# Layer 1's modulation vectors made beside the first parts of two SwiGLU stages; wider context products; more raw buffers in the last SwiGLU

## The chip, the cores and the metric

The kernel runs on one core of a Trainium2 chip. Its engines work side by side, each on its own queue in order: PE (TensorE, matrix products; PEld is its weight load), DVE (VectorE), ACT (ScalarE), POOL (GpSimd) and SP (SyncE, which here only issues transfers). The metric is the device time of one execution in microseconds.

## The reference

Two layers over 512 latent tokens of width 1024 (the noisy x) and 256 context tokens. Each layer is a SwiGLU half step, a mixer, and a second SwiGLU half step:

```
mod_l = silu(c) @ w_mod[i] + b_mod[i]          # 9 vectors of 1024 for the latent stream
mod_c = silu(c_ctx) @ w_mod[i] + b_mod[i]      # and 9 for the context stream
h = rmsnorm(s, g) * (1 + mod[k0 + 1]) + mod[k0]
s = s + 0.5 * mod[k0 + 2] * ((silu(h @ w1) * (h @ w3)) @ w2)     # d_ff = 2816
x = x + mod[5] * mixer(...)                    # layer 0: S5 and pooling; layer 1: gated DeltaNet
```

In layer 1 the context needs only vectors 0 to 4, the latent stream all nine. All arithmetic is in float32: a product of two float32 matrices is three PE products of high and low halves (high × high, high × low, low × high), so weights and activations are split into a high part (copied on ACT) and a low part (a subtraction on DVE).

## The kernel before, in words

The streams x and ctx stand together in SBUF as xT, 128 partitions × 8 blocks × 768 tokens (512 latent, 256 context), 24 KB of each partition, 3 MB in all. Six stages follow one another: ffn01, mixer0, ffn02 (layer 0), ffn11, mixer1, ffn12 (layer 1); the code numbers them ph 1 to 6.

The function ffn7 does the stages 3, 4 and 6. Its first part makes h @ w1, h @ w3 by a scheme of seven block products instead of eight. A unit is one block of d_ff: 7 × 12 = 84 PE products of 384 columns (256 in ffn12, where there is no context). Ahead of the units stands eight(), which does the first four slabs with plain products while the sums of blocks (combine(): tiles hr, h7h, h7l) are still being made on DVE and ACT; its inner ctx() does the context columns, two products of 128 columns for the two halves of a block. unit_prep() gets one unit's weights ready: raw slabs of 512 KB come by SP's queue, ACT makes whi and sh, DVE makes wlo, sl and sums in place. A raw buffer (three of them, RAWS) is loaded again as soon as DVE's sl has read it. The finished units (cffn, with the gate product gkffn for two of them) are stored to DRAM by POOL's queue (gdffn<-cffn).

The second part multiplies by w2 in chunks of units: first units 19 and 20, which have stayed in SBUF (gk), then 0 to 8, 9 to 15, and a last one. It loads the stored units again on POOL's queue (grffn<-gdffn), splits them (ghffn on ACT, glffn on DVE), and DVE adds each result, times the gate, to xT (xT<-ps,gate,xT). PE writes to eight banks; a block of the output takes two of them (one for x, one for ctx) until DVE has added it.

The modulation vectors of layer 1 come from mods(): a slab of w_mod (wm, 512 KB, by POOL's queue), and for each stream one DVE product with a running sum (mscr<-wm,cbc, 128x1024), where cbc holds silu(c) and silu(c_ctx) in every partition. The thread aside() makes them in the second parts of ffn02 (vectors 1, 0, 2, 4, both streams) and of ffn11 (3 for both streams, then 5, 7, 6, 8 for the latent stream), in a pool that has room only there; the main thread waits for ("mods", ph) before the last chunk, because that memory is needed for h.

What stands where on each queue is worked out in advance by class Flow, which runs the threads against a cost model: each has a priority (main work 0 to 4, aside 5), and mods() has a pace in ns (MPS) for its slabs. All engine calls go through one proxy, so the profile has one line, L207, for all of them; tile names tell them apart. In the profile's names the buffer numbers are left out.

Of the kernel before, what the change touches and what calls it, by code (L numbers as in the profile page):

```python
# [10 lines left out]
F32 = mybir.dt.float32  # L11
# [7 lines left out]
P = 128  # L19
# [50 lines left out]
MPS = 4000.0  # L70
RAWS = 3
# [212 lines left out]
class Kern:  # L284
# [47 lines left out]
    def start_stream(self, order):  # L332
        self.order = order
        self.raw, self.sl = {}, {}
        self.pos = 0
        for i in range(RAWS):
            self.slab_dma(i)
        for i in range(3):
            self.slab_prep(i)

    def slab_dma(self, i):
        if i >= len(self.order):
            return
        src, j = self.order[i]
        n = self.A[src].shape[2]
        t = self.slabp.tile([P, 1024], F32, name=f"raw{i}", tag="raw", bufs=RAWS)
        self.nc.sync.dma_start(t[:, :n], self.A[src][j])
        self.raw[i] = (t, n)

    def slab_prep(self, i):  # L350

        if i >= len(self.order):
            return
        src, j = self.order[i]
        if src in UNITS and 2 * CU <= j < 2 * NF:
            if j % 2 == 0:
                self.flow.spawn(self.unit_prep(i), name="slab", prio=3)
            else:
                self.flow.set("slot", i)
            return  # L360

        def prep():
# [12 lines left out]
            self.slab_dma(i + RAWS)  # L375
            self.flow.set("raw", i + RAWS)

        def g():
            if i >= RAWS:
                yield ("raw", i)  # L380
            yield from prep()
        self.flow.spawn(g(), name="slab", prio=3)


    def unit_prep(self, i):
# [47 lines left out]
        for k in range(2):  # L433
            self.slab_dma(i + RAWS + k)
            flow.set("raw", i + RAWS + k)
# [85 lines left out]
    def mods(self, layer, items, bufs, pace, streams=lambda k: (0, 1), beside=None, side="right"):  # L521
# [3 lines left out]
        with self.tc.tile_pool(name=f"mod{layer}{flat[0][1]}", bufs=1, side=side) as mp:  # L525
            cbc = mp.tile([P, 2, D], F32, name="cbc")
# [3 lines left out]
            def load(i):  # L530
                if i < len(flat):
                    _, k, d = flat[i]
                    w[i] = mp.tile([P, D], F32, name=f"wm{layer}_{k}_{d}", tag="wm", bufs=bufs)
                    nc.gpsimd.dma_start(w[i], A["wmod"][layer, 8 * k + d])
# [10 lines left out]
            for i, (gi, k, d) in enumerate(flat):  # L545
                yield self.flow.landed(w[i])
# [3 lines left out]
                for s in streams(k):  # L550
                    scr = mp.tile([P, D], BF16, name="mscr", tag="mscr", bufs=1)
# [15 lines left out]
    def mods_of(self, layer, ks, streams=lambda k: (0, 1), pace=5000.0, beside=None, side="right"):  # L567
        return self.mods(layer, [[(k, d) for d in range(KD)] for k in ks], 2, pace, streams, beside, side)
# [364 lines left out]
    def ffn7(self, layer, which, with_ctx, ph, nxt):  # L933
# [10 lines left out]
        cs, cp = self.cs, self.cp  # L944
        ss = ExitStack()
# [4 lines left out]
        def eight():  # L950
# [4 lines left out]
            def mm(out, u, k, i, cs):  # L955

                w, r = ws[u], blk[k // 4][i]
                t = (k + 4) % 8 if u % 2 == 0 else k
                self.mm3(out, w, t, self.h, (ALL, r, k % 4, cs), k == 0, k == KD - 1)

            def x(us, i):
                for k in range(KD):
                    yield from self.flag("h", ph, i, k)
                    for u in us:
                        mm(px[u][:, i * HN:(i + 1) * HN], u, k, i, slice(0, HN))
                        yield "PE"

            def ctx(u):
# [237 lines left out]
        for c in range(3):  # L1206
            fs, nf = WCH[c], len(WCH[c])
            for d in range(KD):
                px = yield from self.get()
                pc = (yield from self.get()) if with_ctx else None  # L1210
                for i in range(nf):
# [12 lines left out]
                    yield "PE"  # L1224
                yield from self.flag("mod", layer, 3 * n + 2, d)
# [4 lines left out]
        if ph in (3, 4):  # L1230
            yield ("mods", ph)
# [22 lines left out]
        es[1].close()  # L1254

# [1321 lines left out]
    def aside(self):  # L2577
# [9 lines left out]
        yield ("second", 3)  # L2587
        yield from self.mods_of(1, (1, 0, 2, 4), pace=MPS, side="left")
        self.flow.set("mods", 3)
        yield ("second", 4)  # L2590
        yield from self.mods_of(1, (3,), pace=MPS, side="left")
        yield from self.mods_of(1, (5, 7, 6, 8), one, pace=MPS / 2, side="left")
        self.flow.set("mods", 4)
# [188 lines left out]
```

## Time and profile before

| | |
|---|---|
| median of 3 runs | 3070.82 us (3068.51 to 3077.32) |
| profiled execution, its own time | 3083.76 us |
| its span, mean granted clock | 3082.0 us, 0.957 |
| PE busy | 2830.7 us (92%) |
| DVE busy | 2073.8 us (67%) |
| ACT busy | 1244.5 us (40%) |
| ffn02: first part, second part | 1005 to 1298, 1298 to 1504 us |
| ffn11: first part, second part | 1557 to 1852, 1852 to 2065 us |
| ffn12: first part, second part | 2712 to 2940, 2940 to 3067 us |

The time outside the span is 1.8 us. The chain that ended last tells which engine set the end; a window gives one stretch: its length, the busy time of PE, PEld, DVE, ACT and POOL with the number of instructions in brackets, then the granted PE clock as a share of full speed, the busy share of the DMA engines and GB/s. The clock has two levels, 1.2 and 2.4 GHz, so 0.5 is the lower one throughout. A wait names the engine that stood, what it was about to write, and the engine and tile that released it. A PE product is listed from its issue to its modelled end, and the next one starts before that, so the distance of starts is what one costs.

### The profile page before, as it was taken

What the parts mean: (1) busy time and instruction counts of PE and PEld (TensorE: products, weight loads), DVE (VectorE), ACT (ScalarE), POOL (GpSimd) and SP (SyncE); (2) the same over time, 40 slices, a digit from 0 to 9 for tenths busy, and PEclk for the clock granted to TensorE, in tenths of its full rate; (3) what the DMA queues carried; (4) which work ended last, traced back from release to release, by engine and by line L of the source; (5) the groups of instructions that cost most, each with busy time, mean ns of one, the idle gap of its engine ahead of it and who ended that gap; (6) DMA issues with size and microseconds to landing.
All of it is one profiled execution on the core that took longest, in us unless ns stands there. A gap on an engine that the chain in (4) does not pass through costs nothing.

```text
span 3082.0 us, 47486 instructions
## 1 busy us (share of the span) xinstructions
PE 2830.7 (92%) x18572; PEld 2569.6 (83%) x18572; DVE 2073.8 (67%) x3941; ACT 1244.5 (40%) x2464; POOL 707.6 (23%) x1206
## 2 busy tenths in 40 slices
PE   7999899999999999999799999988678888889998
PEld 3778778898888999988799998787567777789977
DVE  6888763366737666588766667667667676687854
ACT  3221212234235444421544443126565766455532
POOL 1343530031311000011200001132664474100011
PEclk9999999999997999999899999989889999899999
DMA  6545442223411223366132326642111123234442
GB/s 226 169 151 171 161 125 64 62 65 92 117 50 36 98 94 99 107 232 196 42 101 95 99 98 222 225 146 78 56 42 45 36 100 111 72 93 123 131 156 74
DMA packets 98673, 343.86 MB, mean 112 GB/s; under 512 B 12384, under 2 KB 16128, under 8 KB 97296
## 3 DMA queue, kind: packets, MB, share of 16 engines
q1 hardware_dynamic: 57552, 192.12, 19.5%
q0 software_dynamic: 37568, 144.51, 14.3%
q10 hardware_dynamic: 3328, 4.20, 0.4%
q8 instruction: 146, 2.39, 0.3%
q14 instruction: 79, 0.65, 0.1%
HBM read 301.81 MB, written 38.96 MB: 111 GB/s over the span
## 4 chain that ended last, share of the span: by engine, by line
PE 60%; DVE 10%; DMA 9%; POOL 9%; issue 8%; ACT 3%; POOLq 0%; DVEq 0%; SPq 0%; ACTq 0%
PE ps L207 60%; DMA wm<-in_wmod_dram 3%; POOL xm L207 2%; POOL s5l L207 2%; POOL z L207 2%; DVE mscr L207 2%; DMA E<-gd 2%; DMA grffn<-gdffn 1%; POOL s5u L207 1%; DVE wlo L207 1%; DMA wf<-in_wmodf_dram 1%; DVE xT L207 1%; DMA z<-in_s5c_dram 1%; DMA og<-ogd 1%; DVE rsq_r L207 1%
## 5 line engine op out<-in xcount | busy, mean ns | idle before, releaser
L207 DVE TENSOR_TENSOR wlo<-raw,whi 128x1024 fp32r<-128x1024 f32 (+1 forms) x310 | 353.6, 1142 | 305.0 <-ACT whi L207 304.6
L207 ACT ACTIVATE whi<-raw 128x1024 fp32r<-128x1024 f32 (+1 forms) x324 | 315.9, 977 | 583.8 <-PE ps L207 530.3
L207 PE MATMUL ps<-hhi,whi 128*128 128x256 f32 (+1 forms) x1304 | 457.2, 351 | 0.5 <-ACT gg L207 0.5
L207 PE MATMUL ps<-hlo,whi 128*128 128x256 f32 (+1 forms) x1304 | 441.3, 338 | 1.1 <-DVE hlo L207 1.1
L207 PE MATMUL ps<-hhi,wlo 128*128 128x256 f32 (+1 forms) x1304 | 440.4, 338 | 2.1 <-DVE wlo L207 1.4
L207 DVE SCALAR_TENSOR_TENSOR mscr<-wm,cbc 128x1024 bf16<-128x1024 f32 x224 | 285.6, 1275 | 62.2 <-DMA wm<-in_wmod_dram 52.8
L207 PE MATMUL ps<-ghffn,whi 128*128 128x256 f32 (+1 forms) x896 | 302.2, 337 | 25.0 <-DVE xT L207 18.2
L207 PE MATMUL ps<-h7h,wlo 128*128 128x384 f32 (+2 forms) x1040 | 319.7, 315 | 4.0 <-DVE wlo L207 4.0
L207 PE MATMUL ps<-h7h,whi 128*128 128x384 f32 (+2 forms) x1040 | 321.4, 317 | 1.2 <-ACT cffn L207 0.8
L207 PE MATMUL ps<-h7h,sl 128*128 128x384 f32 (+1 forms) x960 | 295.0, 319 | 14.1 <-DVE sl L207 14.1
L207 PE MATMUL ps<-glffn,whi 128*128 128x256 f32 (+1 forms) x896 | 301.1, 336 | 1.3 <-DVE glffn L207 1.3
L207 PE MATMUL ps<-ghffn,wlo 128*128 128x256 f32 (+1 forms) x896 | 299.6, 334 | 1.4 <-DVE wlo L207 1.4
L207 PE MATMUL ps<-h7h,sh 128*128 128x384 f32 (+1 forms) x960 | 295.9, 319 | 4.2 <-ACT cffn L207 4.2
L207 PEld LDWEIGHTS ps<-hhi,wlo 128*128 128x128 f32 x1304 | 251.2, 193 | 31.3 <-DVE wlo L207 1.8
L207 PEld LDWEIGHTS ps<-hhi,whi 128*128 128x128 f32 x1304 | 252.2, 193 | 27.3 <-issue 1.4
L207 PEld LDWEIGHTS ps<-hlo,whi 128*128 128x128 f32 x1304 | 252.5, 194 | 25.1 <-DVE hlo L207 1.8
L207 DVE SCALAR_TENSOR_TENSOR xT<-ps,gate,xT 128x256 f32<-128x256 f32 (+1 forms) x352 | 194.2, 577 | 84.6 <-PE ps L207 82.9
L207 PE MATMUL ps<-h7l,whi 128*128 128x384 f32 (+2 forms) x1040 | 240.1, 315 | 2.3 <-DVE h7l L207 2.3
L207 PEld LDWEIGHTS ps<-ghffn,whi 128*128 128x128 f32 x896 | 172.9, 193 | 44.8 <-DVE xT L207 16.5
L207 PEld LDWEIGHTS ps<-h7h,wlo 128*128 128x128 f32 x1040 | 205.7, 198 | 4.5 <-DVE wlo L207 4.4
L207 PEld LDWEIGHTS ps<-h7h,whi 128*128 128x128 f32 x1040 | 206.1, 198 | 2.0 <-ACT cffn L207 1.2
L207 PEld LDWEIGHTS ps<-h7h,sl 128*128 128x128 f32 x960 | 180.7, 188 | 16.4 <-DVE sl L207 16.3
(343 smaller groups left out, 6184.8 us busy)
## 6 DMA issues: line engine op xcount, KB each, us to landing
raw<-in_ffn_dram SPq DMA_DIRECT2D x264, 512.0 KB
wm<-in_wmod_dram POOLq DMA_DIRECT2D x128, 512.0 KB, 4.0
raw<-in_gin_dram SPq DMA_DIRECT2D x33, 512.0 KB
grffn<-gdffn POOLq DMA_DIRECT2D x40, 384.0 KB, 4.5
gdffn<-cffn POOLq DMA_DIRECT2D x36, 384.0 KB, 2.6
wf<-in_wmodf_dram POOLq DMA_DIRECT2D x16, 512.0 KB, 7.8
E<-gd SPq DMA_DIRECT2D x16, 384.0 KB
grffn<-gdffn POOLq DMA_DIRECT2D x20, 256.0 KB, 4.0
```

Of the source, the lines that this page charges most:

```text
L207: r = f(*a, **k)
```

## The change

There are three edits. First, mods_in_x(): once combine() has read xT, POOL writes xT to DRAM (xd), and its memory serves as cbc, three slab buffers and the product's output. In ffn02's first part the vectors 1, 0, 2 are made (pace 9000 ns), in ffn11's first part 4 and 3 for both streams (4500 ns) and 5, 7, 6, 8 for one (2700 ns). Then POOL loads xT back, and the second part waits for ("x", ph) ahead of its first addition to xT. The second parts make no vectors any more. Second, ctx() does both halves of a block in one product of 256 columns, a strided slice of h. Third, ffn12 opens a raw buffer pool of its own with five buffers; slab_dma() counts its slabs itself.

```diff
-MPS = 4000.0
-RAWS = 3
+MPS = 9000.0
...
+        self.rawp, self.raws, self.rawpos = self.slabp, 3, 0
+        for _ in range(self.raws):
+            self.slab_dma()
...
+    def mods_in_x(self, ph, parts):
+
+        nc, flow = self.nc, self.flow
+        xd = self.dram.tile([P, KD, NT], F32, name=f"xd{ph}")
+        yield ("combined", ph)
+        nc.gpsimd.dma_start(xd, self.xT)
+        for ks, streams, pace in parts:
+            yield from self.mods(1, [[(k, d) for d in range(KD)] for k in ks], 3, pace, streams,
+                                 at=self.xT.rearrange("p a c -> p (a c)"))
+        nc.gpsimd.dma_start(self.xT, xd)
+        flow.set("x", ph)
...
+                cbc = at[:, :2 * D].rearrange("p (a c) -> p a c", a=2)
...
+                        w[i] = at[:, (2 + i % bufs) * D:(3 + i % bufs) * D]
...
-                    scr = mp.tile([P, D], BF16, name="mscr", tag="mscr", bufs=1)
+                    scr = mp.tile([P, D], BF16, name="mscr", tag="mscr", bufs=1) if at is None else at[:, 5 * D:]
...
+        if ph == 6:
+            self.rawp, self.raws = rs.enter_context(tc.tile_pool(name="raws", bufs=1, side=SIDES[ph][1])), 5
+            for _ in range(2):
+                self.slab_dma()
...
-                for i in range(2):
-                    for k in range(KD):
-                        yield from self.flag("h", ph, 2, k)
-                        o = 2 * HN * (u % 2)
-                        mm(cb[f][:, (u % 2) * HN + i * P:(u % 2) * HN + (i + 1) * P], u, k, i, slice(HN, HN + P))
-                        if k % 2:
-                            yield "PE"
+                for k in range(KD):
+                    yield from self.flag("h", ph, 2, k)
+                    r = blk[k // 4]
+                    mm(cb[f][:, (u % 2) * HN:(u % 2 + 1) * HN].rearrange("p (a c) -> p a c", a=2), u, k,
+                       slice(r[0], r[1] + 1, r[1] - r[0]), slice(HN, HN + P))
+                    if k % 2:
+                        yield "PE"
...
+                if ph != 6 and ("x", ph) not in flow.flags:
+                    yield ("x", ph)
                 yield from self.flag("mod", layer, 3 * n + 2, d)
...
-        if ph in (3, 4):
-            yield ("mods", ph)
...
-        yield ("second", 3)
-        yield from self.mods_of(1, (1, 0, 2, 4), pace=MPS, side="left")
...
+        both = lambda k: (0, 1)
+        yield from self.mods_in_x(3, [((1, 0, 2), both, MPS)])
+        yield from self.mods_in_x(4, [((4, 3), both, 0.5 * MPS), ((5, 7, 6, 8), one, 0.3 * MPS)])
```

The first place is DVE's queue at the end of ffn02's second part, before (mscr is a product for a modulation vector, x2 two in a row, xT<-ps,gate,xT an addition to the stream):

```order
1505 L207 SCALAR_TENSOR_TENSOR mscr,modv_75<-wm_4_2_12950,cbc 128x1024 x2
1506 L207 SCALAR_TENSOR_TENSOR mscr,modv_75<-wm_4_3_12968,cbc 128x1024 x2
1507 L207 SCALAR_TENSOR_TENSOR mscr,modv_75<-wm_4_4_12990,cbc 128x1024 x2
1508 L207 SCALAR_TENSOR_TENSOR mscr,modv_75<-wm_4_5_12996,cbc 128x1024 x2
1509 L207 SCALAR_TENSOR_TENSOR mscr,modv_75<-wm_4_6_13002,cbc 128x1024 x2
1510 L207 SCALAR_TENSOR_TENSOR mscr,modv_75<-wm_4_7_13008,cbc 128x1024 x2
1511 L207 TENSOR_TENSOR modv_75<-modv_75,vecs 128x8
1512 L207 SCALAR_TENSOR_TENSOR normA<-modv_75,vecs 128x8
1513 L207 TENSOR_TENSOR modv_75<-modv_75,vecs 128x8
1514 L207 SCALAR_TENSOR_TENSOR normA<-modv_75,vecs 128x8
1515 L207 SCALAR_TENSOR_TENSOR xT<-ps_13035,gate,xT 128x256
```

The same place in the change:

```order
1519 L206 TENSOR_TENSOR wlo_12735<-raw_12564,whi_12734 128x1024
1520 L206 SCALAR_TENSOR_TENSOR xT<-ps_12694,gate,xT 128x512
1521 L206 SCALAR_TENSOR_TENSOR xT<-ps_12695,gate,xT 128x256
1522 L206 TENSOR_TENSOR wlo_12793<-raw_12622,whi_12792 128x1024
1523 L206 SCALAR_TENSOR_TENSOR xT<-ps_12746,gate,xT 128x512
1524 L206 SCALAR_TENSOR_TENSOR xT<-ps_12747,gate,xT 128x256
1525 L206 SCALAR_TENSOR_TENSOR xT<-ps_12812,gate,xT 128x256
1526 L206 SCALAR_TENSOR_TENSOR xT<-ps_12827,gate,xT 128x256
1527 L206 SCALAR_TENSOR_TENSOR xT<-ps_12842,gate,xT 128x256
```

The twelve products that stood ahead of the additions of the last chunk are gone from here; only the low halves of slabs stand between the additions.

The second place is POOL's queue where ffn11's first part ends, before:

```order
377 L207 DMA gdffn_13489<-cffn_17_15993 128x768
378 L207 DMA gdffn_13489<-cffn_18_16117 128x768
379 L207 DMA grffn_16599<-gdffn_13489 128x768
380 L207 DMA grffn_16605<-gdffn_13489 128x768
381 L207 DMA grffn_16617<-gdffn_13489 128x768
382 L207 DMA gdffn_13489<-cffn_21_16494 128x768
383 L207 DMA grffn_16621<-gdffn_13489 128x768
384 L207 DMA grffn_16635<-gdffn_13489 128x768
385 L207 DMA grffn_16642<-gdffn_13489 128x768
386 L207 DMA grffn_16650<-gdffn_13489 128x768
```

In the change (xT<-in_wmod_dram is a slab's load into the memory of xT):

```order
380 L206 DMA gdffn_13275<-cffn_17_15767 128x768
381 L206 DMA xT<-in_wmod_dram 128x1024 x4
382 L206 DMA gdffn_13275<-cffn_18_15900 128x768
383 L206 DMA xT<-in_wmod_dram 128x1024 x7
384 L206 DMA xT<-xd_11434 128x6144
385 L206 DMA grffn_16413<-gdffn_13275 128x768
386 L206 DMA grffn_16419<-gdffn_13275 128x768
387 L206 DMA grffn_16430<-gdffn_13275 128x768
388 L206 DMA grffn_16432<-gdffn_13275 128x768
389 L206 DMA gdffn_13275<-cffn_21_16299 128x768
390 L206 DMA grffn_16444<-gdffn_13275 128x768
```

Loads of modulation slabs now stand among the stores of the last units, and the reload of xT directly ahead of the first loads of stored units.

The third place is DVE's queue in eight() of ffn11, before (wlo is the low half of a slab, the one in row 1645 that of the fourth slab; hr and h7l of 128x4x128 are sums of context blocks):

```order
1641 L207 TENSOR_TENSOR h7l<-hr_13032,h7h 128x4x256
1642 L207 TENSOR_TENSOR wlo_13969<-raw_13544,whi_13968 128x1024
1643 L207 TENSOR_TENSOR raw_13544<-raw_13544,raw_13547 128x512
1644 L207 TENSOR_TENSOR raw_13547<-raw_13547 128x512
1645 L207 TENSOR_TENSOR wlo_13966<-raw_13246,whi_13965 128x1024
1646 L207 TENSOR_TENSOR wlo_13973<-raw_13547,whi_13972 128x512
1647 L207 TENSOR_TENSOR raw_13547<-raw_13544,raw_13547 128x512
1648 L207 TENSOR_TENSOR raw_13544<-raw_13544,raw_13547 128x512
1649 L207 TENSOR_TENSOR hr_13031<-hr_13031,hr_13032 128x4x128
1650 L207 TENSOR_TENSOR sl_0_14006<-raw_13547,sh_0_14005 128x1024
1651 L207 TENSOR_TENSOR hr_13032<-hr_13034,hr_13032 128x4x128
1652 L207 TENSOR_TENSOR sl_1_14016<-raw_13544,sh_1_14015 128x1024
```

In the change:

```order
1649 L206 TENSOR_TENSOR h7l<-hr_12809,h7h 128x4x256
1650 L206 TENSOR_TENSOR hr_12808<-hr_12808,hr_12809 128x4x128
1651 L206 TENSOR_TENSOR hr_12809<-hr_12811,hr_12809 128x4x128
1652 L206 SCALAR_TENSOR_TENSOR hr_12811<-hr_12808,hr_12811 128x4x128
1653 L206 TENSOR_TENSOR aaffn_13589<-aaffn_13589,ps_13582 128x2x128
1654 L206 SCALAR_TENSOR_TENSOR hr_12810<-hr_12811,hr_12810 128x4x128
1655 L206 TENSOR_TENSOR h7l<-hr_12811,h7h 128x4x128
1656 L206 TENSOR_TENSOR h7l<-hr_12808,h7h 128x4x128
1657 L206 TENSOR_TENSOR h7l<-hr_12809,h7h 128x4x128
1658 L206 TENSOR_TENSOR wlo_13683<-raw_13030,whi_13682 128x1024
1659 L206 TENSOR_TENSOR wlo_13689<-raw_13306,whi_13688 128x1024
1660 L206 TENSOR_TENSOR raw_13306<-raw_13306,raw_13343 128x512
```

The sums of context blocks now stand ahead of the low half of the fourth slab (row 1658) and of those that follow. PE's own order changes only by the merged context products and a few neighbours, and SP's is the same.

## Rows read from the trace of the kernel before

**Rows 1.** The page's chain that ended last, by engine.

```profile
PE 60%; DVE 10%; DMA 9%; POOL 9%; issue 8%; ACT 3%; POOLq 0%; DVEq 0%; SPq 0%; ACTq 0%
```

**Rows 2.** Windows: us, busy us of each engine (instructions), clock, DMA share, GB/s.

```profile
1005.00:1298.00 293.00, 293.00 (x1685) 292.47 (x1685) 188.24 (x258) 130.30 (x202) 9.72 (x18) 1.00 0.30 97
1557.00:1852.00 295.00, 293.34 (x1685) 292.49 (x1684) 189.68 (x260) 130.11 (x202) 9.72 (x18) 1.00 0.29 96
1298.00:1504.00 206.00, 192.27 (x1172) 171.90 (x1170) 165.04 (x286) 54.01 (x76) 41.68 (x72) 0.97 0.56 181
1852.00:2065.00 213.00, 198.30 (x1171) 175.61 (x1170) 144.10 (x240) 54.06 (x71) 50.06 (x81) 0.94 0.59 200
```

**Rows 3.** Waits of PE, 1852 to 2065: total, times, longest.

```profile
PE ps L207 <- DVE xT L207: 7.7, 3, 4.9
PE ps L207 <- ACT ghffn L207: 6.2, 2, 6.1
```

**Rows 4.** Windows around those three stalls, and an undisturbed stretch.

```profile
1870.00:1945.00 75.00, 75.00 (x429) 65.42 (x428) 54.99 (x84) 18.01 (x17) 13.21 (x25) 1.00 0.70 236
1460.00:1482.00 22.00, 10.78 (x68) 10.57 (x67) 15.98 (x32) 4.99 (x12) 5.96 (x10) 0.69 0.34 105
1945.00:1962.00 17.00, 10.11 (x30) 6.94 (x29) 10.18 (x15) 5.06 (x6) 4.79 (x9) 0.60 0.73 264
2020.00:2041.00 21.00, 14.07 (x84) 13.60 (x83) 14.66 (x27) 3.84 (x9) 4.59 (x7) 0.76 0.44 151
```

**Rows 5.** Timeline, DVE and PE, 1454 to 1475: start, length, [idle before <-releaser].

```profile
1454.70 1.22 DVE L207 SCALAR_TENSOR_TENSOR mscr<-wm,cbc 128x1024 bf16<-128x1024 f32 x1
...
1474.11 0.58 PE L207 MATMUL ps<-ghffn,whi 128*128 128x256 f32 x1 [11.22 <-DVE xT L207]
```

**Rows 6.** Timeline, POOL and ACT, 1946 to 1951.

```profile
1946.54 1.07 POOL L207 DMA_DIRECT2D grffn<-gdffn  x2
...
1950.93 0.84 ACT L207 ACTIVATE ghffn<-grffn 128x768 fp32r<-128x768 f32 x1 [12.60 <-DMA grffn<-gdffn]
```

**Rows 7.** Groups of the page, modulation of the whole run.

```profile
L207 DVE SCALAR_TENSOR_TENSOR mscr<-wm,cbc 128x1024 bf16<-128x1024 f32 x224 | 285.6, 1275 | 62.2 <-DMA wm<-in_wmod_dram 52.8
...
wm<-in_wmod_dram POOLq DMA_DIRECT2D x128, 512.0 KB, 4.0
```

**Rows 8.** Window: spill of x by SP after ffn11, beside other transfers.

```profile
2066.20:2076.00 9.80, 8.34 (x49) 7.59 (x48) 8.94 (x32) 3.63 (x7) 3.70 (x3) 0.73 0.91 323
```

**Rows 9.** Windows: context products, then products of 256 columns.

```profile
961.60:993.50 31.90, 29.77 (x147) 29.44 (x147) 14.27 (x27) 9.52 (x24) 0.60 (x1) 0.55 0.09 30
1529.20:1545.40 16.20, 16.20 (x148) 16.20 (x146) 9.78 (x12) 5.47 (x8) 0.58 (x1) 1.00 0.06 25
2781.00:2788.50 7.50, 7.50 (x66) 7.50 (x65) 5.88 (x10) 4.21 (x8) 0.54 (x1) 1.00 0.49 165
```

**Rows 10.** Timeline, DVE and PE, 1542 to 1547.

```profile
1542.37 1.23 DVE L207 TENSOR_TENSOR wlo<-raw,whi 128x1024 fp32r<-128x1024 f32 x1 [0.33 <-ACT whi L207]
1545.08 1.82 DVE L207 TENSOR_TENSOR wlo<-raw,whi 128x1024 fp32r<-128x1024 f32 x2
...
1546.35 0.39 PE L207 MATMUL ps<-h7h,wlo 128*128 128x256 f32 x1 [0.68 <-DVE wlo L207]
```

**Rows 11.** Window of ffn12's first part.

```profile
2712.00:2940.00 228.00, 210.51 (x1724) 205.58 (x1723) 181.16 (x267) 114.45 (x203) 12.42 (x23) 0.99 0.41 125
```

**Rows 12.** Waits of PE and ACT in it.

```profile
PE ps L207 <- DVE sl L207: 14.1, 10, 2.2
ACT whi L207 <- DMA raw<-in_ffn_dram: 7.6, 10, 2.5
```

**Rows 13.** Timeline of one of these stalls: PE, DVE, ACT.

```profile
2779.28 0.39 PE L207 MATMUL ps<-h7h,sl 128*128 128x256 f32 x1 [1.33 <-DVE sl L207]
...
2779.48 1.22 DVE L207 TENSOR_TENSOR sl<-raw,sh 128x1024 fp32r<-128x1024 f32 x1
...
2782.88 0.63 ACT L207 ACTIVATE whi<-raw 128x512 fp32r<-128x512 f32 x1 [0.20 <-DMA raw<-in_ffn_dram]
```

More of the change, by code (lines that the diff above doesn't have):

```diff
@@ L335, in start_stream, with slab_dma @@
         self.pos = 0
-        for i in range(RAWS):
-            self.slab_dma(i)
+        self.rawp, self.raws, self.rawpos = self.slabp, 3, 0
+        for _ in range(self.raws):
+            self.slab_dma()
         for i in range(3):
             self.slab_prep(i)
-    def slab_dma(self, i):
+    def slab_dma(self):
+        i = self.rawpos
+        self.rawpos += 1
         if i >= len(self.order):
@@ L345, in slab_dma @@
         n = self.A[src].shape[2]
-        t = self.slabp.tile([P, 1024], F32, name=f"raw{i}", tag="raw", bufs=RAWS)
+        t = self.rawp.tile([P, 1024], F32, name=f"raw{i}", tag="raw", bufs=self.raws)
         self.nc.sync.dma_start(t[:, :n], self.A[src][j])
         self.raw[i] = (t, n)
+        self.flow.set("raw", i)
     def slab_prep(self, i):
@@ L374, in prep @@
             self.flow.set("slab", i)
-            self.slab_dma(i + RAWS)
-            self.flow.set("raw", i + RAWS)
+            self.slab_dma()
         def g():
-            if i >= RAWS:
+            if ("raw", i) not in self.flow.flags:
                 yield ("raw", i)
@@ L433, in unit_prep @@
         for k in range(2):
-            self.slab_dma(i + RAWS + k)
-            flow.set("raw", i + RAWS + k)
+            self.slab_dma()
     def slab(self, src, j, ahead=0):
@@ L519, in mod_finish, with mods @@
                 nc.vector.tensor_scalar(self.gate[:, layer, n, s, ds], m, 0.5 if n != 1 else 1.0, None, op0=ALU.mult)
-    def mods(self, layer, items, bufs, pace, streams=lambda k: (0, 1), beside=None, side="right"):
+    def mods_in_x(self, ph, parts):
[8 more added lines that the diff above has]
+        flow.set("x", ph)
+    def mods(self, layer, items, bufs, pace, streams=lambda k: (0, 1), beside=None, at=None):
         nc, A, V = self.nc, self.A, self.nc.vector
         flat = [(gi, k, d) for gi, g in enumerate(items) for k, d in g]
-        with self.tc.tile_pool(name=f"mod{layer}{flat[0][1]}", bufs=1, side=side) as mp:
-            cbc = mp.tile([P, 2, D], F32, name="cbc")
+        with ExitStack() as es:
+            if at is None:
+                mp = es.enter_context(self.tc.tile_pool(name=f"mod{layer}{flat[0][1]}", bufs=1, side="right"))
+                cbc = mp.tile([P, 2, D], F32, name="cbc")
+            else:
+                cbc = at[:, :2 * D].rearrange("p (a c) -> p a c", a=2)
             nc.gpsimd.dma_start(cbc, bass.AP(tensor=A["cc"].tensor, offset=A["cc"].offset, ap=[[0, P], [D, 2], [1, D]]))
@@ L532, in load @@
                     _, k, d = flat[i]
-                    w[i] = mp.tile([P, D], F32, name=f"wm{layer}_{k}_{d}", tag="wm", bufs=bufs)
+                    if at is None:
+                        w[i] = mp.tile([P, D], F32, name=f"wm{layer}_{k}_{d}", tag="wm", bufs=bufs)
+                    else:
+                        w[i] = at[:, (2 + i % bufs) * D:(3 + i % bufs) * D]
                     nc.gpsimd.dma_start(w[i], A["wmod"][layer, 8 * k + d])
@@ L545, in mods @@
             for i, (gi, k, d) in enumerate(flat):
-                yield self.flow.landed(w[i])
+                yield self.flow.landed(w[i]) if at is None else self.flow.ready(w[i], "vector")
                 while self.busy:
@@ L565, in mods, with mods_of @@
                 yield ("s5",)
-    def mods_of(self, layer, ks, streams=lambda k: (0, 1), pace=5000.0, beside=None, side="right"):
-        return self.mods(layer, [[(k, d) for d in range(KD)] for k in ks], 2, pace, streams, beside, side)
+    def mods_of(self, layer, ks, streams=lambda k: (0, 1), pace=5000.0, beside=None):
+        return self.mods(layer, [[(k, d) for d in range(KD)] for k in ks], 2, pace, streams, beside)
     def ring(self, tag):
@@ L944, in ffn7 @@
         cs, cp = self.cs, self.cp
+        rs = ExitStack()
+        if ph == 6:
+            self.rawp, self.raws = rs.enter_context(tc.tile_pool(name="raws", bufs=1, side=SIDES[ph][1])), 5
+            for _ in range(2):
+                self.slab_dma()
         ss = ExitStack()
@@ L953, in eight, with mm @@
             px, cb, aa, ws = [], {}, {}, []
-            def mm(out, u, k, i, cs):
-                w, r = ws[u], blk[k // 4][i]
+            def mm(out, u, k, r, cs):
                 t = (k + 4) % 8 if u % 2 == 0 else k
-                self.mm3(out, w, t, self.h, (ALL, r, k % 4, cs), k == 0, k == KD - 1)
+                self.mm3(out, ws[u], t, self.h, (ALL, r, k % 4, cs), k == 0, k == KD - 1)
             def x(us, i):
@@ L964, in x @@
                     for u in us:
-                        mm(px[u][:, i * HN:(i + 1) * HN], u, k, i, slice(0, HN))
+                        mm(px[u][:, i * HN:(i + 1) * HN], u, k, blk[k // 4][i], slice(0, HN))
                         yield "PE"
@@ L1254, in ffn7 @@
         es[1].close()
+        rs.close()
     def s5_const(self):
@@ L2586, in aside @@
             return
-        yield ("second", 3)
-        yield from self.mods_of(1, (1, 0, 2, 4), pace=MPS, side="left")
[L2589 to L2593, printed above, removed]
+        both = lambda k: (0, 1)
+        yield from self.mods_in_x(3, [((1, 0, 2), both, MPS)])
+        yield from self.mods_in_x(4, [((4, 3), both, 0.5 * MPS), ((5, 7, 6, 8), one, 0.3 * MPS)])
     def body(self, until=None):
```

## The prediction

> **What bounds the kernel now.** I began with the chain that ended last: 60% of the span is PE, the rest is spread over DVE, DMA and POOL [rows 1]. The time is therefore PE's own work plus stalls of PE, so the next view was a table of windows by stage, then PE's waits in the stages that the diff touches, then a timeline at each wait.
>
> The windows show two kinds of stage in ffn02 and ffn11 [rows 2]. In the first parts PE is busy for 293.00 of 293 us and 293.34 of 295 us at a clock of 1.00, while DVE works 188 and 190 us: PE is the bound, and DVE has over 100 us free. In the second parts (206 and 213 us) PE idles 13.7 and 14.7 us and the clock falls to 0.97 and 0.94. That is where the modulation vectors of layer 1 are made in the kernel before. ffn12's first part is 228 us with PE busy 210.51 [rows 11].
>
> **Part 1: the modulation leaves the second parts.** In ffn02 PE stands 11.22 us for an accumulate into xT; DVE had been working through modulation products (mscr, 1.22 us each) since 1454.70 [rows 5], and ten of them stand in its order directly ahead of that accumulate. In ffn11 there are three more waits for xT, 7.7 us together, and 6.1 us for ghffn [rows 3]; that one waits for a grffn load issued only at 1946.54, behind a modulation load on POOL's queue [rows 6].
>
> What the stalls cost, clock included, comes from the windows around them [rows 4]. A product of 256 columns takes 0.117 us at full clock (7.50 us by 64, two of the 66 rows having been in flight at the edge) [rows 9]; the alternating 512 and 256 columns of the longer chunks take 75/429 = 0.175 us on average [rows 4]. So the 68 products in 1460 to 1482 need 8.0 of 22 us: 14.0 lost. The 30 in 1945 to 1962 need 5.3 of 17: 11.7 lost. The 84 in 2020 to 2041 need 9.8 of 21: 11.2 lost. Sum 36.9 us, part of it run at the lower clock level (0.69, 0.60 and 0.76 in these windows) after the wait. With the modulation gone the accumulates and the grffn loads have only each other ahead of them. What is late next is the splitting of grffn (glffn), a few tenths at a time; I leave 3 us for that: **−34**. Bounds: −37, and −25 if a wait of 6 us on grffn stays in each stage.
>
> **Part 2: the same work in the first parts.** 24 slabs for two streams in ffn02 are 48 products; ffn11 gets 16 slabs for two and 32 for one, 64 products. By the page a product takes 1275 ns on DVE and 0.28 us of waiting (62.2/224), nearly all for its slab, which lands 4.0 us after its issue [rows 7]. DVE's work rises from 188.2 to 249.4 of 293 us (85%) and from 189.7 to 271.3 of 295 us (92%); with the waits of ffn11's 64 products, 18 us, to 289 (98%). It still fits, and PE is what hides it. But DVE runs its queue in order, and a product put ahead of a slab's low half delays PE by up to 1.6 us once the lead is used up. I take **+4** (1 and 3). Bounds 0 and +18, the 64 waits uncovered.
>
> The spill of x and its reload are 3 MB each. SP's spill after ffn11 ran with the transfers beside it at 323 GB/s [rows 8], so 3 MB take some 10 us. The spill lies beside a first part whose DMA share is 0.30 [rows 2]: nothing. The reload gates the first accumulate of the second part. In ffn11 it is issued when the last product is done, which stands among the sums of the last unit with two of seven partial products still to run: 24 × 293/1685 = 4 us before the unit's end. So xT is back some 6 to 8 us after the second part has begun. Its first chunk takes 96 products, 16.8 us, for eight blocks of two banks each; four blocks fill the eight banks, so PE runs 8.4 us before it needs one accumulated. If that cover goes, each us later is a us of PE. ffn02's reload lies three units earlier in POOL's order. **+2**, bounds 0 and +9. The grffn loads stand behind the reload on POOL, but are needed only after the 16.8 us.
>
> The rows say of the queue that a grffn load behind a modulation load kept PE for 6.1 us [rows 3, 6]. The Trainium skill (DMA: Bandwidth & Descriptors, SWDGE vs HWDGE vs iDMA) states that a single software queue is allocated, which speaks against putting 3 MB ahead of those loads; its fit in the section on the anatomy of one DMA, 2.0 us plus bytes by 436e3, would give an estimated 9.2 us for them. By that rule the reload holds back the loads as well as the accumulates, which is rival B below.
>
> **Part 3: context halves in one product.** Both stages run 192 products of 128 columns, which become 96 of 256. At full clock one of 128 takes 16.2/146 = 0.111 us, nearly what one of 256 takes, 0.117 [rows 9]. So 21.3 us become 11.2: 10.1 a stage.
> In ffn02 the 144 of the first three units run at a clock of 0.55 for 31.9 us [rows 9]. If the clock rises when it did before, what follows takes the slow time over: 10. If it stays low only for this work, 16 + 2.5. I take **−10**.
> In ffn11 the clock is 1.00 and the work has cover to lose: PE already waits 0.68 us for the fourth slab's low half [rows 10], and the planner now puts seven combining operations of 512 elements ahead of it on DVE, 4.3 us at half of the 1.23 us that 1024 take [rows 10]. PE is done 7.6 us sooner, DVE some 3 us sooner, so unit 3 starts 3 us earlier; the last 48 save 2.5 behind it. **−5**, bounds 0 and −10.
>
> On the width, the row shows 0.111 us for 128 columns. The Trainium skill (TensorE: Matmul & The Clock Gate, Back-to-back issue gap) gives about 81 ns as the sustained spacing at N=128; an estimate with it would be 192 × 0.081 − 11.2 = 4.4 us a stage, so the sum for both would be about 4 us short of mine where the clock is full. This trace disagrees, and the measurement decides.
>
> **Part 4: five raw buffers in ffn12.** Ten waits for sl, every second unit, cost PE 14.1 us, and ACT waits 7.6 us for raw slabs, ten times [rows 12]. One cycle: PE waits 1.33 us, DVE's sl ends at 2780.7 and so frees a raw buffer, and ACT starts on the next slab at 2782.88, the moment it lands [rows 13]. With two more buffers the slab is there before. What is late next is DVE itself, 181 us [rows 11], 84% of 215. I take **−13**. Bounds: −6 if sums and low halves on DVE keep half of it; −20, since 1724 × 0.117 = 202 of 228 us is all that PE needs and the rest has waits of its own.
>
> **Sum.** −34 + 4 + 2 − 10 − 5 − 13 = −56. The profiled execution took 3083.76 us for a span of 3082.0, so 3028 on its basis. It lies 0.42% above the median of 3070.82; scaled by that, 3028 becomes **3015 us**. For this forecast alone 3004 to 3027.
>
> **Rivals.**
> A: DVE takes the place of what is removed. ffn12's cycle is one of DVE and ACT rather than of the buffer, and ffn11's fourth slab comes no earlier. For: DVE is at 79% there and its sl is the named releaser; against: ACT's wait for the raw slab in the same cycle. −34 − 10 + 6 = −38: 3033 us.
> B: POOL's queue is the new wait. Loads that wait for DVE hold the stores and loads behind them, the last product comes 10 us late, and the reload lands 12 us after the banks are full, with 3 us at the lower clock: 15 in each stage. For: 32 loads and the reload stand on one queue with the stores in ffn11's later half. Against: three slab buffers where two were. −56 − 2 + 30 = −28: 3043 us.
> C: everything comes: −37, −19 and −6 for the context, −20, no cost: −82: 2989 us.
> D, slower: DVE becomes the bound of the first parts. The place is DVE's queue, where each of 112 products holds the low halves and sums behind it; the price is 1.56 us each, 175 us in all. It decides against the change from 0.6 us each, which is 67 us, the 58 of gain without part 2's cost and the measurement's 9 on top. At half, 87 us, the sum is −60 + 87 = +27: 3098 us. For: ten in a row cost PE 11.2 us before. Against: in the first parts slabs are prepared ahead and 100 us of DVE are free.
>
> **How the numbers follow.** The forecast has 0.58, A 0.15, B 0.13, C 0.07, D 0.07. 0.3% is 9 us, about what a measurement of this kernel tells from no change. Under 3062: the forecast, A, C and nearly all of B, less mixtures in which several costs meet: 0.87 faster, 0.06 within, 0.07 slower. The range of 2992 to 3045 leaves out C's end and D with the worse half of B.
>
> **What would show it.** Right: no PE wait over 1 us for xT or ghffn in the second parts, 206 and 213 us becoming about 191; first parts at 293 to 298 us with DVE at 85 and 92%; context work halved in rows and 5 us shorter in ffn11, with a new wait for wlo of some 5 us; ffn12's first part at 215 us and no ACT wait for raw. Wrong: PE waits for wlo, sl or cffn in the first parts (D), an idle stretch at the start of a second part that ends with xT or ghffn (B), or waits for sl in ffn12 as long as before (A).

## The result and the profile after

The changed kernel takes 3001.61 us in the median of 4 runs (2999.02 to 3003.67), before 3071.49 us: a ratio of 0.977, with a 95% interval of 0.9753 to 0.9787. A second set on another occasion gave 0.9762 (0.9747 to 0.9777). The forecast was 3015 in a range of 2992 to 3045, with 3004 to 3027 for the forecast alone: the result lies in the range, and 2 us below that narrower one. The sign holds, and so does the size of most parts; one term, the context products of ffn02, was forecast at less than half of what it turned out to be, and the raw buffers came out right for other reasons than those given.

The table gives the length of each stretch in the profiled executions (us). A stretch begins at the first product behind the small products of a stage's norm; a few products that run ahead of those are not counted (six in ffn02 everywhere, and six in ffn11 where the modulation has moved, some 0.7 us). "first" includes the first four slabs, "second" of ffn02 ends at the norm of ffn11, "second" of ffn12 at the last norm. The stretches up to ffn02 and mixer1 run the same code in all kernels and differ by 8 and 6 us between executions; that is what one stage of one execution is uncertain by, mixer1 above all. The profiled execution of before is 12 us above its median, so differences against its row come out large: the two spans differ by 84.8 us where the medians differ by 69.9.

| kernel | up to ffn02 | ffn02 first | second | ffn11 first | second | mixer1 | ffn12 first | second |
|---|---|---|---|---|---|---|---|---|
| before | 943.2 | 355.0 | 206.0 | 341.6 | 217.6 | 617.9 | 252.8 | 133.8 |
| changed | 940.7 | 336.7 | 190.1 | 335.6 | 194.8 | 612.0 | 234.4 | 138.7 |
| merge alone | 941.8 | 331.5 | 206.2 | 335.7 | 216.0 | 614.7 | 251.3 | 132.6 |
| merge made twice | 940.3 | 343.5 | 203.9 | 339.0 | 214.9 | 614.3 | 250.4 | 133.2 |
| modulation alone | 938.4 | 359.6 | 190.1 | 341.1 | 194.9 | 613.9 | 255.5 | 133.5 |
| raw buffers alone | 944.1 | 355.6 | 206.3 | 342.0 | 213.3 | 613.2 | 234.9 | 137.3 |
| without the merge | 936.1 | 360.0 | 190.1 | 341.3 | 194.4 | 617.9 | 234.9 | 137.3 |

The chain that ended last now has 66% of PE and 6% of DMA, where it had 60% and 9% [rows 1].

The windows of the changed kernel, columns as in [rows 2]: the first parts of ffn02 and ffn11, then their second parts.

```profile
984.00:1277.00 293.00, 289.89 (x1661) 288.41 (x1660) 239.53 (x362) 127.23 (x199) 24.12 (x45) 1.00 0.48 165
1515.00:1809.40 294.40, 293.88 (x1695) 293.56 (x1694) 258.78 (x400) 131.47 (x204) 37.25 (x70) 1.00 0.59 206
1277.40:1467.00 189.60, 188.89 (x1172) 169.26 (x1170) 88.40 (x144) 52.37 (x76) 25.67 (x39) 1.00 0.32 103
1809.40:2000.00 190.60, 189.42 (x1173) 169.43 (x1173) 87.29 (x135) 50.10 (x69) 28.25 (x39) 1.00 0.33 112
```

The reader is to see three things. DVE's work has moved: 239.5 and 258.8 us stand in the first parts, 88 and 87 us in the second. PE is busy through 99% of the second parts, at a clock of 1.00 where it was 0.97 and 0.94. And ffn11's first part, with DVE at 88%, still keeps PE busy for 293.88 of 294.40 us.

What is left of PE's waits for xT and ghffn in ffn11's second part [rows 3] is none; these are all its waits there:

```profile
PE ps L206 <- DVE wlo L206: 0.6, 1, 0.6
PE ps L206 <- DVE glffn L206: 0.4, 1, 0.4
```

The reload of xT, in the timeline of POOL and DVE at the end of ffn11's first part: issued at 1804.68, 4.7 us ahead of the second part (1809.4), and there by 1815.3, 5.9 us into it. DVE waits 2.94 us for it, PE not at all.

```profile
1804.68 0.53 POOL L206 DMA_DIRECT2D xT<-xd  x1 [9.26 <-DVE gate L206]
...
1815.32 1.80 DVE L206 SCALAR_TENSOR_TENSOR xT<-ps,gate,xT 128x512 f32<-128x512 f32 x3 [2.94 <-DMA xT<-xd]
```

### The profile page after: what moved, and what is told of

It is laid out like the page before. It is cut to its first block, busy times and chain, and to the rows that moved or that the text cites. A ratio compares the mean times of both kernels' runs of the same rounds, so it can differ in the third digit from the quotient of the medians.

```text
span 2997.2 us, 47031 instructions
## 1 busy us (share of the span) xinstructions
PE 2774.2 (93%) x18380; PEld 2520.0 (84%) x18380; DVE 2060.3 (69%) x3941; ACT 1242.2 (41%) x2464; POOL 708.5 (24%) x1210
## 4 chain that ended last, share of the span: by engine, by line
PE 66%; DVE 10%; POOL 9%; issue 6%; DMA 6%; ACT 3%; POOLq 0%; DVEq 0%; SPq 0%; ACTq 0%
PE ps L206 66%; POOL xm L206 2%; POOL s5l L206 2%; POOL z L206 2%; DMA E<-gd 2%; DVE wlo L206 1%; POOL s5u L206 1%; DVE mscr L206 1%; DMA wf<-in_wmodf_dram 1%; DVE xT L206 1%; DMA grffn<-gdffn 1%; DVE rsq_a L206 1%; DVE nt L206 1%; DMA z<-in_s5c_dram 1%; DVE h7l L206 1%
## 5 line engine op out<-in xcount | busy, mean ns | idle before, releaser
L206 PE MATMUL ps<-h7h,whi 128*128 128x256 f32 (+1 forms) x976 | 298.6, 314 | 4.6 <-ACT whi L206 4.0
L206 PE MATMUL ps<-h7h,wlo 128*128 128x256 f32 (+1 forms) x976 | 297.4, 313 | 4.9 <-DVE wlo L206 4.8
L206 PE MATMUL ps<-h7l,whi 128*128 128x256 f32 (+1 forms) x976 | 217.9, 313 | 2.1 <-DVE h7l L206 2.1
L206 ACT ACTIVATE cffn<-ps 128x384 f32<-128x384 f32 (+1 forms) x300 | 131.7, 451 | 197.6 <-PE ps L206 196.4
L206 POOL TENSOR_TENSOR sqsum<-sqsum,sq 128x256 f32<-128x256 f32 x96 | 78.2, 815 | 557.8 <-ACT sq L206 476.4
L206 PEld LDWEIGHTS ps<-h7h,wlo 128*128 128x128 f32 x976 | 188.2, 193 | 6.0 <-DVE wlo L206 5.7
L206 PEld LDWEIGHTS ps<-h7h,whi 128*128 128x128 f32 x976 | 188.2, 193 | 5.5 <-ACT whi L206 4.4
L206 PEld LDWEIGHTS ps<-ghffn,wlo 128*128 128x128 f32 x896 | 169.2, 189 | 23.7 <-DVE wlo L206 6.7
```

The lines of the kernel that those rows point to most:

```text
L206: r = f(*a, **k)
```

## The experiments

### The merge alone

```diff
 before, with the change's mm() and ctx() in eight()
+                    mm(cb[f][:, (u % 2) * HN:(u % 2 + 1) * HN].rearrange("p (a c) -> p a c", a=2), u, k,
+                       slice(r[0], r[1] + 1, r[1] - r[0]), slice(HN, HN + P))
```

> The kernel before with only the context halves merged (96 products of 256 columns a stage instead of 192 of 128). By the working of the prediction: 10 us in ffn02 and 5 us in ffn11, so 15 us less, about 3056 on a median of 3071. Theory K: the long stretch at the lower clock in ffn02 of before (31.9 us at 0.55) belongs to the narrow products themselves and goes with them, then ffn02 gains 16 + 2.5 = 18 and the whole 23 to 25 us, about 3047. In the changed kernel the stretch of context work and the first four slabs was 18.2 us shorter, which speaks for K. Rival G: the clock fell because of the waits for h7l and would come back at its own time; then 10 + 5.

3044.86 us, ratio 0.9917 (0.9903 to 0.993): 25.5 us less (21 to 30). ffn02's first part lost 23.5 us, ffn11's 5.9. That is the size that theory K gives; the next run tests it against G.

### As many products, each twice as wide

```diff
 merge alone, with
-                for k in range(KD):
+                for k in [k for _ in range(2) for k in range(KD)]:
```

> The kernel before with the merged product made twice over, so 192 products of 256 columns a stage: as many products as before, each twice as wide, with the second pass writing the same result again. No PE work is saved: at full clock 192 x 0.117 = 22.5 us against 192 x 0.111 = 21.3 us before, 1.2 us more a stage. Theory K (narrow products keep the clock low in ffn02): the 144 products of ffn02 run at full clock in about 17 us instead of 31.9, so the kernel gains some 12 us, about 3059, without any product less. Rival G (the clock comes back at its own time after the waits for h7l): the 30 us at the lower clock stay and the time is 3071 to 3075, no gain.

3055.75 us, ratio 0.9955 (0.9941 to 0.9969): 13.8 us less (10 to 18) without one product less. In the kernel before 144 products took 31.9 us at a clock of 0.55 [rows 9]. Here all 144 took 20.9 us (958.82 to 979.71). These are 17.5 and 31.9 us from shortly behind where they begin (PE alone: busy, clock, DMA share, GB/s):

```profile
959.50:977.00 17.50, 15.68 (x117) 0.90 0.02 7
959.50:991.40 31.90, 30.08 (x241) 0.95 0.18 63
```

And the waits of PE around that place, 955 to 980, in this kernel:

```profile
PE ps L207 <- DVE h7l L207: 1.7, 2, 0.9
```

The same view of the kernel before:

```profile
PE ps L207 <- DVE h7l L207: 2.1, 2, 1.2
```

Both have two short waits for h7l, and the clock falls beside them in both. With products of 128 columns it stayed at the lower level for the rest of the work; with 256 columns it was 0.95 over the same 31.9 us. The stretch at the lower level in the kernel before (columns as in [rows 2]):

```profile
964.80:995.52 30.72, 29.80 (x140) 29.61 (x140) 12.45 (x21) 7.24 (x16) 0.60 (x1) 0.50 0.09 31
```

Every kernel of this case shows the same split. Where the products have 128 columns, this stretch lasts 30.7 us (before, modulation alone, raw buffers alone) or 34.1 us (without the merge) and ends 2.4 to 5.5 us behind the last of the 144. Where they have 256 columns it lasts 3.4 us (this kernel, and every one that has both the merge and the moved modulation), and in the merge alone it does not come at all, though PE waited 1.9 us for h7l there. The waits differ a little (the longest is 1.1 to 1.2 us with narrow products, 0.9 us with wide ones), but in sum the changed kernel waits longer, 2.5 us against 2.1 before.

The 48 narrow products that come later in the same stage of before ran at 1.00 (1000.0 to 1005.2), and so did those of ffn11 [rows 9], where PE did not wait between the norm and their end. So narrow products alone did not lower the clock; once it had fallen they did not bring it back. The rival, a clock that returns at its own time, falls. What decides whether it falls at all is not shown.

### The modulation alone

```diff
 before, with mods_in_x(), the changed mods() and the wait for ("x", ph)
+        yield from self.mods_in_x(3, [((1, 0, 2), both, MPS)])
+        yield from self.mods_in_x(4, [((4, 3), both, 0.5 * MPS), ((5, 7, 6, 8), one, 0.3 * MPS)])
```

> The kernel before with only the modulation of layer 1 moved beside the first parts (xT in DRAM meanwhile). By the prediction -34 + 4 + 2 = -28, about 3043. Theory now, from the changed kernel's second parts (190 us and 195 us instead of 206 and 218, to the first products of mixer1): -16 and -23, with at most 3 us given back in the first parts: -36 to -39, about 3034. The rival that DVE is the bound of the first parts would show first parts over 300 us, and under 20 us gained.

3044.5 us, ratio 0.9919 (0.9904 to 0.9934): 24.9 us less (20 to 29). By stages the second parts lose 15.9 and 22.7 us and ffn02's first part takes 4.6 more, 34 in all. The stages say more than the timing's interval allows; mixer1 and ffn12, whose code is the same, vary by some us between executions, and which of the two is nearer stays open. That ffn11's first part costs nothing (341.1 against 341.6) and ffn02's does is seen in both kernels with the old context products.

Where ffn02's cost is, in the changed kernel's timeline of DVE and PE: the first modulation product stands in DVE's queue 5.86 us, until ACT has made silu(c) in xT's memory, which had to wait for the spill. The sums behind it are late, and PE waits for sl. This is read from the trace; no run took that product out of the way.

```profile
1006.28 1.23 DVE L206 SCALAR_TENSOR_TENSOR xT<-xT 128x1024 f32<-128x1024 f32 x1 [5.86 <-ACT xT L206]
...
1016.54 0.45 PE L206 MATMUL ps<-h7h,sl 128*128 128x384 f32 x1 [1.33 <-DVE sl L206]
```

A second such wait of 1.6 us follows; these two are all of PE's waits behind the first four slabs (984 to 1277), and the kernel with the modulation alone has the same two (3.0 us).

### Five raw buffers alone

```diff
 before, with slab_dma() counting for itself, and
+            self.rawp, self.raws = rs.enter_context(tc.tile_pool(name="raws", bufs=1, side=SIDES[ph][1])), 5
```

> The kernel before with only the five raw buffers in ffn12. By the prediction -13, about 3058: the ten waits for sl go. The rival that the cycle is one of DVE and ACT rather than of the buffer would leave at least half of the 14 us of waits for sl, -6 or less.

3061.56 us, ratio 0.9969 (0.996 to 0.9979): 9.5 us less (6 to 12). ffn12's first part lost 17.9 us, its second took 3.5 more. In the changed kernel PE's waits in the first part are (2616 to 2660, then nothing until the second part):

```profile
PE ps L206 <- ACT cffn L206: 6.8, 1, 6.8
PE ps L206 <- DVE wlo L206: 3.3, 1, 3.3
...
```

All ten waits for sl [rows 12] are gone. The 3.3 us at the start were there before; the 6.8 us are new, and so is most of this in the second part (2851 to 2978):

```profile
PE ps L206 <- DVE wlo L206: 4.9, 2, 3.1
...
```

### The changed kernel again, and three kernels beside it

The base has no edit.

> The changed kernel once more, as the base for the three kernels beside it on the same chip: 0.977 of before, about 3001.

3002.48 us, ratio 0.9762. The first of the three gives the slabs' buffers back earlier:

```diff
 changed kernel, eight()
                     evac(u, False)
-            for _ in range(3):
-                self.slab_done()
+                    self.slab_done()
+            else:
+                for _ in range(3):
+                    self.slab_done()
```

> The changed kernel, with the buffer of each of the first three slabs of a stage given back after that slab's own context products instead of after all three. Theory: the new 5.2 us of PE waits in ffn11 (3.7 for whi, 1.5 for wlo of the fourth slab) come from that slab's halves being made only when all context products are through, so they go: 5 us less than the changed kernel, about 2996. Rival: DVE's sums of context blocks are what is late; then the wait only changes its name, to h7l or to wlo of the next unit, and the time stays within 2 us.

2991.25 us, ratio 0.9729 (0.9715 to 0.9743). PE's waits from 1481 to 1809, ffn11's first part, in the changed kernel:

```profile
PE ps L206 <- ACT whi L206: 3.7, 1, 3.7
PE ps L206 <- DVE wlo L206: 1.5, 1, 1.5
...
```

In this kernel (1474 to 1799):

```profile
PE ps L206 <- ACT cffn L206: 2.0, 1, 2.0
...
```

The 5.2 us are gone and 2.0 have come; the first parts are 1.8 and 3.2 us shorter than those of the base (334.7 against 336.5, 332.3 against 335.5). That is 5 us by stages; the timed 11 us contain 6 that no stage of the change explains.

The run does not separate its two theories, though. In the changed kernel PE stands from 1500.20, when the context products are through, but ACT makes the fourth slab's whi only at 1502.79, behind high copies of context sums, for the first of which it had waited for DVE:

```profile
1500.80 0.63 ACT L206 ACTIVATE h7h<-hr 128x512 fp32r<-128x512 f32 x1 [4.22 <-DVE hr L206]
...
1502.79 2.51 ACT L206 ACTIVATE whi<-raw 128x1024 fp32r<-128x1024 f32 x3
```

DVE then makes wlo at 1504.82, behind the last low half of these sums. Here, with the early return, wlo stands at 1491.05 and the first sum of 512 elements at 1495.92: the edit gives the buffer back sooner and also puts the slab ahead of the sums. As whi and wlo take 1.0 and 1.2 us, an estimate is that some 2 of the 5.2 us belong to the late return alone and 3 to the sums.

The second has more buffers for reloaded units:

```diff
-        pr = es[0].enter_context(tc.tile_pool(name=f"gr{src}", bufs=4, side=side))
+        pr = es[0].enter_context(tc.tile_pool(name=f"gr{src}", bufs=8 if ph == 6 else 4, side=side))
```

> The changed kernel with eight instead of four buffers for reloaded units (grffn) in ffn12's second part. Theory: the 4.9 us of PE waits for wlo there, new with the five raw buffers, come from ACT standing in its queue for a grffn load that was issued late for want of a buffer, with whi behind it; they go, 3 to 5 us less than the changed kernel. Rival: the loads are slow because raw slabs share the DMA engines; then more buffers change nothing, within 2 us.

2993.7 us, ratio 0.9736 (0.9719 to 0.9754). ffn12's second part is 132.9 us instead of 137.9 in the base, so the 5 us that the raw buffers had moved there come back (the timing says 9). ACT's waits for grffn in it, first in the changed kernel (the kernel before had 11.2 us in 4):

```profile
ACT ghffn L206 <- DMA grffn<-gdffn: 16.5, 8, 5.1
```

With eight buffers:

```profile
ACT ghffn L206 <- DMA grffn<-gdffn: 6.7, 4, 3.7
```

Then both:

> The changed kernel with both, the early return of the first slabs' buffers and eight grffn buffers in ffn12: the two gains lie in different stages and add up, 8 to 10 us less than the changed kernel, about 2992.

2989.49 us, ratio 0.972 (0.9704 to 0.9736): 13 us less than the base, and the lowest median of all, though its interval overlaps that of the early return alone. By stages it is 2.1 + 4.7 + 5.8 = 12.6 us (334.4, 330.8 and 132.1 us). By their own timings the two would have given 11 + 9 = 20, so for gains of this size the stages are the better measure.

### More products than DVE has room for

```diff
-        yield from self.mods_in_x(4, [((4, 3), both, 0.5 * MPS), ((5, 7, 6, 8), one, 0.3 * MPS)])
+        yield from self.mods_in_x(4, [((4, 3), both, 0.5 * MPS), ((5, 7, 6, 8), both, 0.3 * MPS)])
```

> The changed kernel with vectors 5 to 8 of layer 1 made for the context stream too, which nobody reads: 32 more products on DVE in ffn11's first part, 41 us where the changed kernel's DVE has 294.4 - 258.8 = 35.6 us free. In the planner's order 12 of the loads then stand behind the first part. Theory: PE's units stay at 294 us, as DVE's extra work is put where it is free, and the price comes all at the reload of xT: 12 slabs of two products, 12 x 2.6 = 31 us, and 10 us of reload less the 8.4 us of cover, some 33 us, with part of it at the lower clock: 35 to 45 us more than the changed kernel, about 3042. Rival D: the units themselves stretch, to over 300 us, since low halves and sums wait behind the products.

3067.34 us, ratio 0.9982 (0.997 to 0.9993): 65 us more than the changed kernel, nearly all the gain. The units did not stretch (297 us with PE busy for 295.82, its only waits 0.7 and 0.5 us):

```profile
1518.00:1815.00 297.00, 295.82 (x1712) 295.18 (x1711) 262.76 (x404) 130.75 (x204) 30.32 (x57) 1.00 0.52 178
...
1889.65 0.79 PE L206 MATMUL ps<-gkffn,whi 128*128 128x512 f32 x1 [58.93 <-DVE xT L206]
```

The price came at the reload, as expected in kind, but 59 us of it instead of some 33, and 65 in all where 35 to 45 were expected: the loads and products left over run one behind the other, and the reload goes out at 1878.5.

### A slower pace

```diff
-        ... ((5, 7, 6, 8), one, 0.3 * MPS)])
+        ... ((5, 7, 6, 8), one, 0.36 * MPS)])
```

> The changed kernel with a slower pace for the last 32 products of ffn11 (3240 instead of 2700 ns a slab), so that the last of them and the reload come up to 17 us later. In the changed kernel the reload was issued 4.7 us before the second part began and landed 5.9 us into it, 2.5 us before the 8.4 us of cover end by the working of the prediction. Theory: only what exceeds that shows on PE. If the reload comes 10 us later PE stops for some 7 us, 12 us with the lower clock at most; the first part is unchanged.

3035.57 us, ratio 0.9883 (0.9867 to 0.9898): 33 us more than the changed kernel. The reload came 35 us later, not 17, and ffn11's second part is 227.7 us instead of 194.8:

```profile
1837.27 0.54 POOL L206 DMA_DIRECT2D xT<-xd  x1 [8.87 <-DVE modv L206]
...
1848.43 0.80 PE L206 MATMUL ps<-gkffn,whi 128*128 128x512 f32 x1 [33.15 <-DVE xT L206]
```

The second part began at 1806.8 and PE's wait at 1815.3, so the eight banks lasted 8.5 us (the prediction's cover was 8.4). 30.5 us to the issue, and 10.2 to the landing, less 8.5 are 32.2: every microsecond beyond the cover is one of PE. The second part is 32.9 us longer, so the lower clock behind the wait cost nothing that shows here. That the reload came twice as late as the pace alone gives lies in POOL's queue: the last modulation slab was issued at 1827.87, behind eleven loads of stored units (from 1808.82 on), most of which waited until DVE's glffn had freed a buffer. That is rival B's queue.

### Four raw buffers instead of five

```diff
-            self.rawp, self.raws = rs.enter_context(tc.tile_pool(name="raws", bufs=1, side=SIDES[ph][1])), 5
+            self.rawp, self.raws = rs.enter_context(tc.tile_pool(name="raws", bufs=1, side=SIDES[ph][1])), 4
```

> The changed kernel with four raw buffers in ffn12 instead of five. One unit takes two slabs, and a slab takes about 2 us to land. Theory: with four, one unit's two slabs can land while the two before are worked on, so the waits for sl are gone already and ffn12's first part stays within 2 us of 234.5. Rival: DVE's lead needs the fifth; then a part of the 14 us of waits comes back, 3 to 8 us.

3003.98 us, ratio 0.9776 (0.9763 to 0.9789), ffn12's first part 235.0 us: the fifth buffer brings nothing that can be measured.

### Without the merge

```diff
 changed kernel, with the old mm() and ctx() of eight()
```

> The changed kernel with the context products of 128 columns as before, so modulation and raw buffers together without the merge. Alone, the merge took 25.5 us off, the modulation 24.9 and the buffers 9.5, 60 together, where all three take 70. If the parts only add up, this one is 70 - 25 = 45 us below before, about 3026. If the merge is worth more beside the moved modulation it is above 3031; less, below 3021.

3031.24 us, ratio 0.987 (0.9854 to 0.9886): 40 us below before, so the merge is worth 30 beside the other two, and 23.3 + 5.7 = 29.0 by stages (360.0 and 341.3 us in the table). Alone it was 29.4 by stages. By stages the parts add up; the timings lie within their intervals of that.

## Why the prediction was right, and where not

**The second parts (−34).** Right: −15.9 in ffn02 and −22.8 in ffn11, 38.7, which is past my bound of −37. The stalls and their time at the lower clock went whole. The 3 us left over for splitting grffn were not needed (1.0 us of waits). ffn11's second part was 1.6 to 4.3 us longer in the profiled execution of before than in three kernels that share its code, so 2 or 3 us of the 22.8 are chance, and some 36 are left.

**The first parts (+4).** Right in sum, wrong in place. I gave 1 us to ffn02 and 3 to ffn11, by DVE's share of busy time. ffn02 paid 4.6 to 5.0, of which 2.9 are the two waits for sl behind a first product that waited for its own input; where the other 2 come from is not shown. ffn11 paid nothing that can be seen, at a DVE share of 88% (forecast 92%; ffn02 82%, forecast 85%). What can be traced to a cause is an instruction placed ahead of its data, not the load of the engine.

**The reload (+2).** Right in mechanism and times (6 to 8 us forecast, 5.9 measured; cover 8.4, measured 8.5), with a cost of nothing here. Rival B's wait does not occur in the changed kernel, but it is real: with the slower pace and the overload it is 33 and 59 us in one stage, a microsecond for each one past the cover. The reload's 10.6 us (1804.68 to 1815.32) are 1.4 more than the 9.2 us estimated from the Trainium skill (DMA: Bandwidth & Descriptors, anatomy of one DMA). The Trainium skill (DMA: Bandwidth & Descriptors, SWDGE vs HWDGE vs iDMA) has a single software queue, and the trace agrees that loads behind the reload come later: the first took 7.2 us to land here (1809.86 to 1817.09) and 3.2 in ffn02, where the reload had long landed. That cost PE nothing, as forecast: 16.8 us of products stand before the first of them is needed.

**The context products (−10 and −5).** ffn11 was right: −5.9, with a new wait of 5.2 us. I named DVE's combining sums as its cause. They are a part of it, through ACT's queue as much as DVE's (3.7 of the 5.2 us are for whi, which ACT makes); the other part, which I had not seen, is that the fourth slab could not begin before all context products were through. The early return undoes both at once. ffn02 was mis-sized: −23 instead of −10. The step that failed is "if the clock rises when it did before, what follows takes the slow time over: 10"; I had the other end, 16 + 2.5, beside it and took the lower. The run with products twice as wide shows that the slow time belonged to the narrow products. Neither end of my bounds held that: the wide products were not only half as many, they also ran at full clock. At full clock the 72 products of the first three units take 8.4 us; in the merge alone they took 12.0 us at a clock of 1.00, 2.3 us of it short waits (columns as in [rows 2]):

```profile
960.40:972.40 12.00, 9.74 (x75) 8.83 (x74) 11.42 (x24) 9.42 (x23) 0.60 (x1) 1.00 0.00 1
```

So 31.7 us (961.64 to 993.36) became 12.0, which is 20 us; with the 2.5 us of the fourth slab's products and about 1 us of products behind them that had begun at the lower clock, that makes the 23.5. In the changed kernel the 72 took 13.4 us, 3.4 of them at the lower level.

**The raw buffers (−13).** Right in sum, and by luck: −18 in the first part, +3.5 to +4.9 given back in the second, so −13.5 to −14.4 by stages and −9.5 timed. The ten waits for sl, 14.1 us, went as forecast. But PE's waits in the whole first part fell only from 21.3 to 10.6 us, since others for cffn fell by 3.4 and the one of 6.8 came; the rest of the 18 is PE's busy time, 231.5 us before and 223.7 after for the same products, which I had not counted. The step "what is late next is DVE itself" was wrong: DVE had room, and what came was ACT standing for grffn in the next part, which eight buffers undid. Why the raw buffers brought those waits is not shown.

**Slips that move nothing.** Twelve modulation products, not ten, stood ahead of the accumulate in ffn02. Rival D's gain without part 2's cost is 60, as its own sum has it, not 58. By the 81 ns the context term would be 8.8 for both stages, some 6 short of my 15 and not 4.

**The rivals.** A fell (no wait for sl was left). B did not come. D, DVE as the bound of the first parts, fell up to a share of 88%; a first part into which the planner is forced to put more was not tried. C, everything without cost, lay as near to the measured time (2989 against 3001.6) as the forecast did (3015): the 14 us that the forecast is off are about what ffn02's context term was short by.

## What to carry to other kernels

Before moving work to where an engine is free, ask what the last piece of it releases: here a wait behind the moved work cost nothing while it ended inside 8.5 us of bank cover, and then a microsecond for each one (33 us in one run). Beside an engine's share of busy time, look at its queue for an instruction that stands ahead of its own data. And when a stretch runs at the lower clock, find out whether the products in it keep it there: widening them may give more than the count of products says.

## What the runs showed of the hardware that was not expected

Once the clock had fallen beside two waits of about 1 us, products of 128 columns ran at 1.2 GHz for as long as they lasted (30.7 to 34.1 us in four kernels); with 256 columns after like waits the lower level lasted 3.4 us or did not come. The same number of products, each twice as wide, made the stage 11.5 us shorter (343.5 against 355.0). At full clock one of 128 columns takes 0.111 us and one of 256 takes 0.117: the narrow ones cost the same and do half.
